# Causal scores of the first 128 queries: high and low key halves as one 256-column product per head, their halves added with the mask on VectorE

## Chip, cores and metric

One core of one Trainium2 chip runs the whole program: two layers of a decoder trunk over 256 tokens. The metric is device time in microseconds (us), the median of several runs of one execution each. The kernel before takes 412.61 us (3 runs, 412.49 to 412.74).

Engines, as the profile names them: PE is TensorE's matmul, PEld its weight load, DVE is VectorE, ACT is ScalarE, POOL is GpSimd, and SP issues most DMAs.

## What is computed

Each layer projects the normalised tokens to seven groups of columns and a gate, runs three branches (block attention, a gated linear recurrence, cross-attention on memory tokens), multiplies by the gate and projects back. The change touches the block attention alone. With 256 tokens and blocks of 256 keys there is one block, so it is causal attention with 8 heads of width 64. Cut to that:

```python
qa = partial_rope(rms_norm(q_a.reshape(B, S, 8, 64), moba_q_norm[l]), positions)
ka = partial_rope(rms_norm(k_a.reshape(B, S, 8, 64), moba_k_norm[l]), positions)
s = jnp.einsum('bhqd,bhld->bhql', qa, ka) * 64 ** -0.5
s = jnp.where(kpos[None, :] <= qpos[:, None], s, -jnp.inf)
o_a = jnp.einsum('bhql,bhld->bhqd', jax.nn.softmax(s, axis=-1), va)
```

## The kernel before

**Precision.** Matmul operands are of type float32r, which keeps fewer bits than float32. So operands are split into a high part (the value cast to float32r) and a low part (the value minus the high part), and a product is the sum of two or three products in PSUM. Every weight chunk (128 x 1024, `wr`) is split so: ACT writes the high part `wh` (line 147), DVE the low part `wl` (line 159). Line 199 is the helper `mm`, through which most products go, so that tiles rather than lines tell them apart.

**Staging.** The main loop walks weight chunks in a fixed order. PE accumulates a projection in `acc` tiles (4 PSUM banks). All else (norms, attention, recurrence) lives in generators, which the main loop advances by a step after each half chunk, and which use `sd` tiles (4 other PSUM banks). A counter `held["sd"]` limits how many `sd` tiles are handed out at a time. The order on each engine is then decided by the framework's scheduler, from the order of the code and its own estimate of durations; at run time each engine works its queue strictly in that order, and an instruction that waits holds up all that is queued behind it.

**The block attention.** `g_qk` makes keys and queries ready: per pair of heads p (4 of them) and parity e (2) the transposed keys, 64 rows per head. For keys (q=1) the high part `kh` and the low part `kl` are written to 64 of 128 partitions and copied by four DMAs on ACT's queue (line 876) to the other 64; for queries the high and low parts lie one above the other in the 128 partitions of `qs`. A product of `qs` (128 rows) with `kh` thus gives (high + low query) times high key, and one with `kl` the same times the low key. `kl` shares its buffers with the output tiles of the memory branch (`yh`, `yl` of branch `M_`), which are written later in a layer.

`g_moba_unit(l, u)` runs once for each parity u, so two units per layer and four in all. It has two steps t, one for each half of the queries:

- t = 0: queries 0 to 127 see keys 0 to 127. For each of 4 heads a 128-column product with `kh` and one with `kl` are summed in PSUM; the 4 heads fill one `sd` tile.
- t = 1: queries 128 to 255 see keys 0 to 255: two 256-column products per head, 4 heads in two `sd` tiles.
- After each step DVE adds the mask `cm` to each head's scores and takes the row maximum in one instruction (line 906; the profile calls it CUSTOM_DVE_ANT_0, and a short READ_ACCUMULATOR follows each). The result goes to `P`.
- Later: the negated scaled maximum `nba` (line 910), the exponentials on ACT (line 919), the reciprocal `ria` of the sums (line 924), the scaling of `P` (line 928), transposes of `P` on PE (line 938), and the product with the values.

Around these steps stand in time the projection of the attention's gate (`acc<-hT,wh` and `acc<-hT,wl`, with `al` copied by ACT at line 282 and `as` added by DVE at line 283), the last levels of the recurrence (`hQ`, `hK`, `hST`, `hX`), and then the projections of the memory gate and of the memory queries.

Of the kernel before, what the change touches and what calls it, by code (L numbers as in the profile page):

```python
# [45 lines left out]
def hymba_kernel(ctx: ExitStack, tc: tile.TileContext, x, mem, mem_t, positions, w_in, w_out, w_mem_kv,  # L46
# [16 lines left out]
    def room(what, n=1):  # L63
        while held[what] + n > room_of[what]:
            yield
# [14 lines left out]
    def rel(what="sd", n=1):  # L80
        held[what] -= n
# [116 lines left out]
    def mm(o, a, b, s, e):  # L198
        nc.tensor.matmul(o, lhsT=a, rhs=b, start=s, stop=e)  # L199
# [482 lines left out]

    def y_tiles(br):
        if f"y{br}" not in T:
            T[f"y{br}"] = [sb.tile([128, 4, 256], F32R, name=f"y{c}{br}", tag=f"y{c}{br}", bufs=1) for c in "hl"]
        return T[f"y{br}"]

    def y_store(l, br, u, po):
# [129 lines left out]
    def g_qk(l, q, acc):  # L818
        ss = small("ssa", 16)
        ms = small("msa", 16)  # L820
        r = small("rka" if q else "rqa", 16)
        kr = sb.tile([128, 2, 512], F32, name="kr", tag="qk", bufs=1)
        for t in range(2):
            t8 = slice(t * 8, t * 8 + 8)
            sumsq(ss[:, t8], acc[t], 8)
            nc.vector.tensor_scalar(ms[:, t8], ss[:, t8], 1.0 / 64, EPS, op0=OP.mult, op1=OP.add)  # L826
            nc.gpsimd.tensor_tensor(r[:, t8], ms[:, t8], pw[:, :8], op=OP.pow)  # L827
            a3 = heads(acc[t], 8)
            k3 = heads(kr[:, t], 8)
            nc.vector.tensor_tensor(k3, a3, rtA[:, l, q, t][:, None, :].to_broadcast([128, 8, 64]), op=OP.mult)  # L830
            tm = sb.tile([128, 8, 16], F32, name="tm", tag="tm", bufs=2)
            nc.vector.tensor_tensor(tm[:, :, 0:8], a3[:, :, 8:16],
                                    rtB[:, l, q, t][:, None, 0:8].to_broadcast([128, 8, 8]), op=OP.mult)
            nc.vector.tensor_tensor(tm[:, :, 8:16], a3[:, :, 0:8],
                                    rtB[:, l, q, t][:, None, 8:16].to_broadcast([128, 8, 8]), op=OP.mult)
            yield
            nc.vector.tensor_tensor(k3[:, :, 0:16], k3[:, :, 0:16], tm, op=OP.add)
            yield
        if q == 0:
            rq = small("rq", 16)  # L840
            nc.gpsimd.tensor_scalar(rq, r, 0.125, None, op0=OP.mult)
            nr = small("nr", 16)
            nc.gpsimd.tensor_scalar(nr, r, -0.125, None, op0=OP.mult)
            T["rq"], T["nr"] = rq, nr
        else:
            yield
            for t in range(2):
                k3 = heads(kr[:, t], 8)
                nc.vector.tensor_tensor(k3, k3, r[:, t * 8:t * 8 + 8][:, :, None].to_broadcast([128, 8, 64]),
                                        op=OP.mult)  # L850
                yield
        yield 2
        halves = (slice(0, 64), slice(64, 128))
        if q:
            hi = [sb.tile([128, 4, 256], F32R, name="kh", tag=f"kh{e}", bufs=1) for e in range(2)]
            lo = [sb.tile([128, 4, 256], F32R, name="kl", tag=f"y{c}{M_}", bufs=1) for c in "hl"]
        else:
            hi = lo = [sb.tile([128, 4, 256], F32R, name="qs", tag=f"y{c}{A_}", bufs=1) for c in "hl"]
        for t in range(2):
            ts = slice(t * 128, (t + 1) * 128)  # L860
            yield from room("sd")
            pt = side_tile()
            for p in range(4):
                nc.tensor.transpose(pt[:, p * 128:(p + 1) * 128], kr[:, t, p * 128:(p + 1) * 128], ident)  # L864
            p3 = heads(pt, 4)
            for e in range(2):
                r = halves[e]
                nc.scalar.copy(hi[e][r, :, ts], p3[r])
                nc.vector.tensor_tensor(lo[e][halves[e if q else 1 - e], :, ts], p3[r], hi[e][r, :, ts].bitcast(F32),
                                        op=OP.subtract)  # L870
            rel()
            yield
        if q:
            for a in (hi, lo):
                for e in range(2):
                    nc.scalar.dma_start(a[e][halves[1 - e]].bitcast(F32), a[e][halves[e]].bitcast(F32))
            T["k2"] = hi, lo
        else:
            T["q2"] = hi
            spawn(g_moba(l))  # L880

    def g_moba_unit(l, u):
        qs, rq, nr = T["q2"][u], T["rq"], T["nr"]
        kh, kl = (a[u] for a in T["k2"])
        yield from room("P")
        held["P"] += 1
        P = sb.tile([128, 4, 384], F32, name="P", tag="P", bufs=2)
        mx = small("mxa%d" % u, 8)
        nb = small("nba%d" % u, 8)
        sm = small("sma%d" % u, 8)  # L890
        ri = small("ria%d" % u, 8)
        kc = (slice(0, 128), slice(128, 384))
        for t in range(2):
            nk = 128 * (t + 1)
            if t:
                yield
            yield from room("sd", t + 1)
            ps = [side_tile() for _ in range(t + 1)]
            ps = [ps[i * nk // 512][:, i * nk % 512:i * nk % 512 + nk] for i in range(4)]
            for i in range(4):  # L900
                for k in (kh, kl):
                    mm(ps[i], qs[:, i, t * 128:(t + 1) * 128], k[:, i, 0:nk], k is kh, k is kl)
            yield
            for i in range(4):
                c = t * 4 + i
                nc.vector.tensor_tensor_reduce(out=P[:, i, kc[t]], in0=ps[i],
                                               in1=cm[:, 256 - nk:], scale=1.0, scalar=-3e38,
                                               op0=OP.add, op1=OP.max, accum_out=mx[:, c:c + 1])
            rel("sd", t + 1)
        nc.vector.tensor_tensor(nb.rearrange("p (t h) -> p t h", t=2), mx.rearrange("p (t h) -> p t h", t=2),  # L910
                                nr.rearrange("p (t h e) -> p t h e", t=2, e=2)[:, :, :, u], op=OP.mult)
        yield
        while u and f"z{M_}{l}" not in done:
            yield
        yield 4
        for t in range(2):
            for i in range(4):
                c, r = t * 4 + i, t * 8 + 2 * i + u
                pin(nc.scalar.activation(P[:, i, kc[t]], P[:, i, kc[t]], AF.Exp, bias=nb[:, c:c + 1],
                                         scale=rq[:, r:r + 1], accum_out=sm[:, c:c + 1]))  # L920
                if i % 2 == 1:
                    yield
        yield
        nc.vector.reciprocal(ri, sm)
        for t in range(2):
            for i in range(4):
                c = t * 4 + i
                nc.vector.tensor_scalar(P[:, i, kc[t]], P[:, i, kc[t]], ri[:, c:c + 1], None, op0=OP.mult)
        yield 2
        tag = ("PTh", "PTl")[u]  # L930
        yield from take(tag)
        PT = sb.tile([128, 4, 384], F32, name="PT", tag=tag, bufs=1)
        for b in range(3):
            bs = slice(b * 128, (b + 1) * 128)
            yield from room("sd")
            pt = side_tile()
            for i in range(4):
                nc.tensor.transpose(pt[:, i * 128:(i + 1) * 128], P[:, i, bs], ident)  # L938
            nc.scalar.copy(PT[:, :, bs], heads(pt, 4))
            rel()  # L940
        rel("P")
        T[f"PT{u}"] = PT
        if u == 0:
            return
        yield 2
        while f"va{l}" not in done or f"z{A_}{l}" not in done:
            yield
        va = T["va"]
        PT = [T.pop(f"PT{e}") for e in range(2)]
        for w in range(2):  # L950
            yield from room("sd")
            po = side_tile()
            for i in range(4):
                p, e = 2 * w + i // 2, i % 2
                h = 2 * p + e
                rows, c = slice(64 * e, 64 * e + 64), (i // 2) * 256
                mm(po[rows, c:c + 256], va[:, 0, h * 64:(h + 1) * 64], PT[e][:, p, 0:256], True, False)
                mm(po[rows, c + 128:c + 256], va[:, 1, h * 64:(h + 1) * 64], PT[e][:, p, 256:384], False, True)
            if w == 0:
                yield  # L960
                y_store(l, A_, w, po)
        rel("PTh")
        rel("PTl")
        yield
        y_store(l, A_, 1, po)
# [234 lines left out]
```

## Time and profile before

| | |
|---|---|
| median of 3 runs | 412.61 us |
| the profiled execution, its own time | 412.44 us |
| its span, first to last instruction | 410.7 us |
| granted TensorE clock, mean | 1.000 |
| products `kh`/`kl` with `qs` of 128 columns | 32 in all, 8 per unit |
| the same of 256 columns | 32 in all, 8 per unit |
| HBM read, written | 66.22 MB, 1.05 MB |

The times of a profiled execution are counted from the start of its span; 1.74 us of its own time lie outside the span. Busy time of PE is no rate: a matmul's row in the trace is longer than the distance to the next matmul's start, since matmuls overlap. What a product costs is therefore read here from starts, or from the chain of waits, which gives back-to-back work as one piece with its whole length. The block attention's scores lie at 113 to 125 us in the first layer and at 313 to 325 us in the second.

### The profile page before, as it was taken

The page shows a single profiled execution, that of the slowest core. Times are in us where ns is not written, and L with a number is a line of the kernel's source. Part 1 is how long each engine was busy: PE and PEld are TensorE (multiplying, and loading weights), DVE is VectorE, ACT ScalarE, POOL GpSimd, SP SyncE. Part 2 cuts the span into 40 slices and gives each one's busy share as a digit, 9 for nine tenths or more (in the row PEclk, how much of TensorE's full clock was granted, in tenths as well). Part 3 has the DMA queues.
Part 4 walks back from the last instruction along what each step waited for, and adds up shares of the span by engine and source line. Part 5 has one row for each costly group of instructions (what it writes and reads, how often), then busy time and mean ns, then how long its engine had stood idle before and what let it go on. Part 6 is the DMA issues. An engine that isn't in the chain of part 4 may idle for free.

```text
span 410.7 us, 7662 instructions
## 1 busy us (share of the span) xinstructions
PE 404.4 (98%) x2940; PEld 338.4 (82%) x2940; DVE 314.6 (77%) x608; ACT 266.6 (65%) x439; POOL 53.1 (13%) x79
## 2 busy tenths in 40 slices
PE   8999999999999999999999999999999999999996
PEld 6788887878899888888878888887888988887885
DVE  4789886788997777876468689659889977678654
ACT  5867864444967999564457666444577599976530
POOL 2005205064001002000000020005400010200000
PEclk9999999999999999999999999999999999999999
DMA  7984666436753444434446555555565434463402
GB/s 253 413 301 134 196 203 194 169 115 213 212 168 119 155 154 155 134 123 153 153 156 204 170 190 166 193 166 174 176 175 188 155 116 143 154 199 107 153 2 102
DMA packets 20261, 69.86 MB, mean 170 GB/s; under 512 B 2560, under 2 KB 2944, under 8 KB 20224
## 3 DMA queue, kind: packets, MB, share of 16 engines
q1 hardware_dynamic: 19296, 67.12, 49.4%
q10 hardware_dynamic: 928, 2.25, 2.2%
q8 instruction: 23, 0.38, 0.4%
q14 instruction: 14, 0.11, 0.1%
HBM read 66.22 MB, written 1.05 MB: 164 GB/s over the span
## 4 chain that ended last, share of the span: by engine, by line
PE 91%; DMA 3%; DVE 3%; ACT 1%; issue 1%; SPq 0%; DVEq 0%
PE acc L199 60%; PE acc L1084 15%; PE sd L199 8%; DMA wr<-in_w_mem_kv_dram 3%; PE sd L203 2%; PE sd L938 1%; PE sd L864 1%; DVE wl L162 1%; PE sd L1047 1%; PE sd L406 1%; ACT wh L150 1%; DVE xs L1118 0%; PE sd L702 0%; PE sd L582 0%; PE sd L993 0%
## 5 line engine op out<-in xcount | busy, mean ns | idle before, releaser
L159 DVE TENSOR_TENSOR wl<-wr,wh 128x1024 fp32r<-128x1024 f32 x104 | 127.1, 1223 | 38.8 <-ACT wh L147 38.3
L147 ACT CAST wh<-wr 128x1024 fp32r<-128x1024 f32 x104 | 109.4, 1052 | 69.7 <-PE acc L199 45.4
L199 PE MATMUL acc<-wh,hT 128*128 128x512 f32 x384 | 122.2, 394 | 0.0
L199 PE MATMUL acc<-hT,wh 128*128 128x512 f32 x256 | 91.5, 398 | 0.3 <-DVE vml L597 0.3
L199 PEld LDWEIGHTS acc<-wh,hT 128*128 128x128 f32 x384 | 71.7, 188 | 14.5
L199 PE MATMUL acc<-wl,hT 128*128 128x512 f32 x192 | 76.2, 397 | 0.0
L199 PE MATMUL acc<-hT,wl 128*128 128x256 f32 x256 | 72.4, 283 | 0.0
L199 PEld LDWEIGHTS acc<-hT,wh 128*128 128x128 f32 x256 | 48.1, 188 | 11.3 <-DVE vml L597 0.7
L199 PEld LDWEIGHTS acc<-hT,wl 128*128 128x128 f32 x256 | 48.4, 189 | 0.2
L199 PEld LDWEIGHTS acc<-wl,hT 128*128 128x128 f32 x192 | 36.1, 188 | 6.9
L1084 PE MATMUL acc<-wl,yh 128*128 128x512 f32 (+1 forms) x96 | 37.3, 394 | 0.0
L1084 PE MATMUL acc<-wh,yl 128*128 128x512 f32 (+1 forms) x96 | 36.9, 393 | 0.0
L1084 PE MATMUL acc<-wh,yh 128*128 128x512 f32 (+1 forms) x96 | 35.2, 397 | 0.0
L162 DVE SCALAR_TENSOR_TENSOR wl<-wr,gT,wh 128x1024 fp32r<-128x1024 f32 (+1 forms) x17 | 20.2, 1220 | 8.7 <-ACT wh L150 8.7
L199 PE MATMUL acc<-wh,mTh 128*128 128x512 f32 x64 | 25.5, 399 | 1.4 <-ACT wh L150 0.9
L150 ACT ACTIVATE wh<-wr,gT 128x1024 fp32r<-128x1024 f32 (+1 forms) x17 | 18.4, 1101 | 12.1 <-PE acc L1084 5.0
L199 PE MATMUL acc<-wh,mTl 128*128 128x512 f32 x64 | 25.0, 390 | 0.0
L827 POOL TENSOR_TENSOR rka<-msa,pw 128x8 f32<-128x8 f32 x4 | 14.2, 3561 | 55.2 <-DVE msa L826 55.2
L1084 PEld LDWEIGHTS acc<-wh,yl 128*128 128x128 f32 x96 | 18.1, 188 | 3.7 <-issue 0.2
L1084 PEld LDWEIGHTS acc<-wl,yh 128*128 128x128 f32 x96 | 18.1, 188 | 3.6 <-issue 0.2
L1084 PEld LDWEIGHTS acc<-wh,yh 128*128 128x128 f32 x96 | 17.9, 188 | 3.8 <-issue 0.3
L199 PE MATMUL acc<-wl,mTh 128*128 128x512 f32 x64 | 20.8, 393 | 0.2 <-DVE wl L162 0.2
(210 smaller groups left out, 615.8 us busy)
## 6 DMA issues: line engine op xcount, KB each, us to landing
wr<-in_w_in_dram SPq DMA_DIRECT2D x80, 512.0 KB, 3.4
wr<-in_w_out_dram SPq DMA_DIRECT2D x24, 512.0 KB, 3.4
wr<-in_w_mem_kv_dram SPq DMA_DIRECT2D x15, 512.0 KB, 3.6
xs<-in_x_dram SPq DMA_DIRECT2D x2, 512.0 KB, 9.2
memr<-in_mem_dram SPq DMA_DIRECT2D x2, 512.0 KB, 6.4
kh<-kh ACTq DMA_DIRECT2D x4, 256.0 KB, 4.5
kl<-kl ACTq DMA_DIRECT2D x4, 256.0 KB, 3.3
out_dram<-xs SPq DMA_DIRECT2D x3, 256.0 KB, 2.0
```

The costliest lines, as they stand in the source:

```text
L147: nc.scalar.copy(whs[i], raws[i])
L150: nc.scalar.activation(whs[i][:, sl], raws[i][:, sl], AF.Copy, scale=gT[:, g:g + 1])
L159: nc.vector.tensor_tensor(wls[i], raws[i], whs[i].bitcast(F32), op=OP.subtract)
L162: nc.vector.scalar_tensor_tensor(wls[i][:, sl], in0=raws[i][:, sl], scalar=gT[:, g:g + 1], in1=whs[i][:, sl].bitcast(F32), op0=OP.mult, op ...
L199: nc.tensor.matmul(o, lhsT=a, rhs=b, start=s, stop=e)
L203: tc.keep_in_program_order(nc.tensor.matmul(o, lhsT=a, rhs=b, start=True, stop=True))
L406: ins = nc.tensor.transpose(pt[:, j * 256 + t * 128:j * 256 + (t + 1) * 128], xn[t][:, k * 128:(k + 1) * 128], ident)
L827: nc.gpsimd.tensor_tensor(r[:, t8], ms[:, t8], pw[:, :8], op=OP.pow)
L864: nc.tensor.transpose(pt[:, p * 128:(p + 1) * 128], kr[:, t, p * 128:(p + 1) * 128], ident)
L938: nc.tensor.transpose(pt[:, i * 128:(i + 1) * 128], P[:, i, bs], ident)
L1047: nc.tensor.transpose(pt[:, i * 256 + t * 128:i * 256 + (t + 1) * 128], P[:, t, i, b * 128:(b + 1) * 128], ident)
L1084: ins = nc.tensor.matmul(a, lhsT=y, rhs=wt[:, cs], start=n == (0 if to is None else nk - 2) and j == 0, stop=n == nk - 1 and j == 2)
```

## The change

The high and low keys of a unit move into one tile `k2` of shape (128, 4 heads, 2 parts, 256 keys): for one head the high part's 256 columns are followed by the low part's 256. At t = 0 one product per head reads columns 0 to 127 of both parts, 256 columns in two runs of 128, and writes (high) and (low) side by side into 256 columns of an `sd` tile. So 4 heads now need two `sd` tiles. For each of them DVE first adds the mask to the low halves of its two heads (a new instruction, 128 partitions x 2 x 128, written to `P`), and the old instruction then adds the high half and `P`, where it added the high half and the mask, and takes the maximum. At t = 1 the same products are computed as before. The DMAs between the halves of the partitions now move 4 runs of 256 floats in each partition where they moved one of 1024. The memory branch's `yh` and `yl` become the halves of one tile `y2` that shares its buffer with the second unit's `k2`.

```diff
     def y_tiles(br):
         if f"y{br}" not in T:
-            T[f"y{br}"] = [sb.tile([128, 4, 256], F32R, name=f"y{c}{br}", tag=f"y{c}{br}", bufs=1) for c in "hl"]
+            if br == M_:
+                y2 = sb.tile([128, 2, 4, 256], F32R, name="y2", tag="y2", bufs=1)
+                T[f"y{br}"] = [y2[:, c] for c in range(2)]
...
         if q:
-            hi = [sb.tile([128, 4, 256], F32R, name="kh", tag=f"kh{e}", bufs=1) for e in range(2)]
-            lo = [sb.tile([128, 4, 256], F32R, name="kl", tag=f"y{c}{M_}", bufs=1) for c in "hl"]
+            k2 = [sb.tile([128, 4, 2, 256], F32R, name="k2", tag=t, bufs=1) for t in ("k2", "y2")]
+            hi, lo = ([a[:, :, c] for a in k2] for c in range(2))
...
-            yield from room("sd", t + 1)
-            ps = [side_tile() for _ in range(t + 1)]
-            ps = [ps[i * nk // 512][:, i * nk % 512:i * nk % 512 + nk] for i in range(4)]
+            yield from room("sd", 2)
+            ps = [side_tile() for _ in range(2)]
             for i in range(4):
-                for k in (kh, kl):
-                    mm(ps[i], qs[:, i, t * 128:(t + 1) * 128], k[:, i, 0:nk], k is kh, k is kl)
+                o, q = ps[i // 2][:, i % 2 * 256:i % 2 * 256 + 256], qs[:, i, t * 128:(t + 1) * 128]
+                if t == 0:
+                    mm(o, q, k2[:, i, :, 0:128], True, True)
+                else:
+                    for c in range(2):
+                        mm(o, q, k2[:, i, c], c == 0, c == 1)
             yield
+            if t == 0:
+                for b in range(2):
+                    nc.vector.tensor_tensor(P[:, 2 * b:2 * b + 2, kc[0]],
+                                            ps[b].rearrange("p (h c s) -> p h c s", h=2, c=2)[:, :, 1],
+                                            cm[:, None, 128:].to_broadcast([128, 2, 128]), op=OP.add)
             for i in range(4):
                 c = t * 4 + i
-                nc.vector.tensor_tensor_reduce(out=P[:, i, kc[t]], in0=ps[i],
-                                               in1=cm[:, 256 - nk:], scale=1.0, scalar=-3e38,
+                o = ps[i // 2][:, i % 2 * 256:i % 2 * 256 + nk]
+                nc.vector.tensor_tensor_reduce(out=P[:, i, kc[t]], in0=o, in1=cm if t else P[:, i, kc[t]],
+                                               scale=1.0, scalar=-3e38,
                                                op0=OP.add, op1=OP.max, accum_out=mx[:, c:c + 1])
-            rel("sd", t + 1)
+            rel("sd", 2)
```

The scheduler orders the engines anew. **PE, first unit of layer 0, before** (out <- operands, the moving tile first; numbers tell tiles of one name apart): the eight 128-column products stand together in tile `sd_1447` within the gate's projection.

```order
L199 MATMUL acc_1481<-hT_159,wh_1324 128x512
L199 MATMUL sd_1447<-kh_1197,qs_1345 128x128
L199 MATMUL sd_1447<-kl_1199,qs_1345 128x128
...
L199 MATMUL acc_1481<-hT_159,wl_1381 128x256
...
L199 MATMUL sd_1490<-kh_1197,qs_1345 128x256
L199 MATMUL sd_1490<-kl_1199,qs_1345 128x256
```

The same place of the changed kernel, down to the first products of the second unit (`k2_1198`):

```order
L199 MATMUL acc_1478<-hT_159,wh_1322 128x512
L199 MATMUL sd_1445<-k2_1197,qs_1343 128x256 x2
L199 MATMUL acc_1478<-hT_159,wl_1379 128x256
...
L199 MATMUL sd_1446<-k2_1197,qs_1343 128x256 x2
L199 MATMUL sd_1487<-k2_1197,qs_1343 128x256 x4
L199 MATMUL sd_1488<-k2_1197,qs_1343 128x256 x4
...
L199 MATMUL sd_1532<-hQ_687,hK_534 128x128 x4
...
L199 MATMUL sd_1544<-k2_1198,qs_1344 128x256 x2
```

Two of the four products of t = 0 (`sd_1445`) stay where the eight were; the other two (`sd_1446`) now stand with those of t = 1. Between the first and the second unit's products 48 `acc` products, 12 `sd` products of 256 columns and the 4 of `hQ`, `hK` are queued. The second unit's `sd_1544` waits for DVE's last reading of `sd_1487`.

**DVE at the same place, before:** after the recurrence's `hK` and a weight split, the four maxima of t = 0 follow one another (a READ_ACCUMULATOR row after each).

```order
L752 TENSOR_TENSOR hK_534<-hK_534,hT32_1385 128x8x64
L159 TENSOR_TENSOR wl_1468<-wr_1322,wh_1416 128x1024
L906 ISA P_1442,mxa0_1443<-sd_1447,cm_162 128x128
...
L283 TENSOR_TENSOR as_1413<-acc_1433,al_1478 128x256
L159 TENSOR_TENSOR wl_1515<-wr_1377,wh_1466 128x1024
L283 TENSOR_TENSOR as_1510<-acc_1481,al_1523 128x256
L906 ISA P_1442,mxa0_1443<-sd_1490,cm_162 128x256
```

**DVE, changed:** the same stretch has the two new additions (line 913), and the maxima of t = 0 (line 919 with `P` as second operand) come in two pairs; the second pair is queued behind t = 1's.

```order
L756 TENSOR_TENSOR hK_534<-hK_534,hT32_1383 128x8x64
L913 TENSOR_TENSOR P_1440<-sd_1445,cm_162 128x2x128
L159 TENSOR_TENSOR wl_1463<-wr_1320,wh_1414 128x1024
L283 TENSOR_TENSOR as_1411<-acc_1431,al_1475 128x256
L919 ISA P_1440,mxa0_1441<-sd_1445,P_1440 128x128
...
L159 TENSOR_TENSOR wl_1512<-wr_1375,wh_1461 128x1024
L283 TENSOR_TENSOR as_1507<-acc_1478,al_1520 128x256
L913 TENSOR_TENSOR P_1440<-sd_1446,cm_162 128x2x128
L919 ISA P_1440,mxa0_1441<-sd_1487,cm_162 128x256
...
L679 TENSOR_TENSOR zT0_169<-as_1411,sg_1497 128x512
L919 ISA P_1440,mxa0_1441<-sd_1446,P_1440 128x128
```

**DVE some 25 us later, changed:** the reciprocal of the first unit's sums, which waits for ACT's exponentials, now stands ahead of the weight split `wl_1770`, and the eight scalings of `P` behind it. Before, that split (`wl_1774`) stood behind the eight scalings.

```order
L159 TENSOR_TENSOR wl_1736<-wr_1612,wh_1697 128x1024
L812 SCALAR_TENSOR_TENSOR zh_168<-sd_1583,hgr_1650,zh_168 128x128 x4
L812 SCALAR_TENSOR_TENSOR zh_168<-sd_1618,hgr_1650,zh_168 128x128 x4
L937 RECIPROCAL ria0_1444<-sma0_1443 128x8
L283 TENSOR_TENSOR as_1694<-acc_1711,al_1747 128x256
L159 TENSOR_TENSOR wl_1770<-wr_1662,wh_1734 128x1024
L941 TENSOR_SCALAR P_1440<-P_1440,ria0_1444 128x128 x4
```

The moves around the reciprocal change the place of DVE's work, not its amount.

More of the change, by code (lines that the diff above doesn't have):

```diff
@@ L684, in y_tiles @@
         if f"y{br}" not in T:
-            T[f"y{br}"] = [sb.tile([128, 4, 256], F32R, name=f"y{c}{br}", tag=f"y{c}{br}", bufs=1) for c in "hl"]
+            if br == M_:
+                y2 = sb.tile([128, 2, 4, 256], F32R, name="y2", tag="y2", bufs=1)
+                T[f"y{br}"] = [y2[:, c] for c in range(2)]
+            else:
+                T[f"y{br}"] = [sb.tile([128, 4, 256], F32R, name=f"y{c}{br}", tag=f"y{c}{br}", bufs=1) for c in "hl"]
         return T[f"y{br}"]
@@ L876, in g_qk @@
                     nc.scalar.dma_start(a[e][halves[1 - e]].bitcast(F32), a[e][halves[e]].bitcast(F32))
-            T["k2"] = hi, lo
+            T["k2"] = k2
         else:
@@ L883, in g_moba_unit @@
         qs, rq, nr = T["q2"][u], T["rq"], T["nr"]
-        kh, kl = (a[u] for a in T["k2"])
+        k2 = T["k2"][u]
         yield from room("P")
@@ L896, in g_moba_unit @@
                 yield
-            yield from room("sd", t + 1)
-            ps = [side_tile() for _ in range(t + 1)]
-            ps = [ps[i * nk // 512][:, i * nk % 512:i * nk % 512 + nk] for i in range(4)]
+            yield from room("sd", 2)
+            ps = [side_tile() for _ in range(2)]
             for i in range(4):
-                for k in (kh, kl):
-                    mm(ps[i], qs[:, i, t * 128:(t + 1) * 128], k[:, i, 0:nk], k is kh, k is kl)
-            yield
+                o, q = ps[i // 2][:, i % 2 * 256:i % 2 * 256 + 256], qs[:, i, t * 128:(t + 1) * 128]
+                if t == 0:
+                    mm(o, q, k2[:, i, :, 0:128], True, True)
+                else:
+                    for c in range(2):
+                        mm(o, q, k2[:, i, c], c == 0, c == 1)
+            yield
+            if t == 0:
[3 more added lines that the diff above has]
+                                            cm[:, None, 128:].to_broadcast([128, 2, 128]), op=OP.add)
             for i in range(4):
                 c = t * 4 + i
-                nc.vector.tensor_tensor_reduce(out=P[:, i, kc[t]], in0=ps[i],
-                                               in1=cm[:, 256 - nk:], scale=1.0, scalar=-3e38,
+                o = ps[i // 2][:, i % 2 * 256:i % 2 * 256 + nk]
+                nc.vector.tensor_tensor_reduce(out=P[:, i, kc[t]], in0=o, in1=cm if t else P[:, i, kc[t]],
+                                               scale=1.0, scalar=-3e38,
                                                op0=OP.add, op1=OP.max, accum_out=mx[:, c:c + 1])
-            rel("sd", t + 1)
+            rel("sd", 2)
         nc.vector.tensor_tensor(nb.rearrange("p (t h) -> p t h", t=2), mx.rearrange("p (t h) -> p t h", t=2),
```

## The prediction

> **What bounds the kernel now.** First the page: busy time, the chain of waits by engine, and the view of who kept PE waiting.
>
> ```profile
> span 410.7 us, 7662 instructions
> PE 404.4 (98%) x2940; PEld 338.4 (82%) x2940; DVE 314.6 (77%) x608; ACT 266.6 (65%) x439; POOL 53.1 (13%) x79
> PEclk9999999999999999999999999999999999999999
> PE 91%; DMA 3%; DVE 3%; ACT 1%; issue 1%; SPq 0%; DVEq 0%
> ...
> PE sd L199 <- DVE dm L325: 1.0, 1, 1.0
> PE acc L199 <- ACT wh L150: 0.9, 2, 0.5
> PE acc L199 <- DVE xs L1118: 0.5, 1, 0.5
> PE acc L199 <- DVE vml L597: 0.3, 1, 0.3
> PE acc L199 <- DVE wl L162: 0.2, 1, 0.2
> ```
>
> PE is busy for 404.4 of 410.7 us, the chain that ended last is PE's own for 91%, and in the whole span PE waited 2.9 us for anybody, none of it for the attention. The granted clock is full in every slice. So what PE no longer executes leaves the end, as long as nobody makes PE wait instead. The busy times by stretch (layer 0; columns PE, PEld, DVE, ACT, POOL, then clock, DMA share, GB/s) show who could:
>
> ```profile
> 108.00:126.00 18.00, 18.00 (x133) 16.18 (x132) 17.78 (x48) 12.55 (x24) 0.00 (x0) 1.00 0.54 167
> 126.00:148.00 22.00, 22.00 (x129) 19.00 (x127) 17.43 (x41) 20.44 (x38) 1.67 (x1) 1.00 0.43 136
> 148.00:160.00 12.00, 12.00 (x58) 9.94 (x57) 6.95 (x10) 11.93 (x25) 2.39 (x2) 1.00 0.48 153
> ```
>
> PE is full in all three. But in the stretch where the change adds work to DVE, DVE is busy for 17.78 of 18.00 us, and ACT is nearly full in the two behind it. These are the places to watch.
>
> **What PE loses.** The chain in order of time (start, length, what) has the eight products of t = 0 of both units, and in between the first unit's eight of t = 1, as pieces of their own:
>
> ```profile
> 113.29 0.84 PE sd L199 x8
> 114.13 3.58 PE acc L199 x20
> 117.71 0.94 PE sd L199 x8
> 118.65 0.46 PE acc L199 x3
> 119.11 0.89 PE sd L199 x8
> 120.00 0.93 PE acc L199 x5
> 120.93 0.84 PE sd L199 x8
> ...
> 312.96 0.84 PE sd L199 x8
> 320.61 0.84 PE sd L199 x8
> ```
>
> Eight products of 128 columns take 0.84 us, 0.105 each; eight of 256 columns take 0.94, 0.117 each. Twice the columns cost a ninth more. The reason stands in the tile's groups: every product has a weight load of its own, of the same 190 ns whatever follows, and these come no closer than about 0.11 us.
>
> ```profile
> L199 PEld LDWEIGHTS sd<-kl,qs x32: 187/189/192, 113.1 to 324.8; 128*128 128x128 f32 x32
> L199 PE MATMUL sd<-kl,qs x32: 272/278/285, 113.2 to 325.0; 128*128 128x128 f32 x16, 128*128 128x256 f32 x16
> ```
>
> Four products of 256 columns take 4 x 0.117 = 0.47 us, so a unit saves 0.84 - 0.47 = 0.37 us, and four units 1.48. From below, the 256 columns now come in two runs of 128, and no row shows a moving operand of that form: if each run cost what a product of its own does, the saving would be 0. From above, a product cannot save more than it costs: 16 x 0.105 = 1.68. I take 1.48, since only 16 of 32 weight loads are left, and the 256-column row is the nearest. Splitting t = 0 into two places costs nothing that the rows show, since `sd` and `acc` products follow each other at every border above without a gap.
>
> Here a rule of the Trainium skill can be held against the rows. Its page "TensorE: Matmul & The Clock Gate", section "Back-to-back issue gap", has an isolated matmul at columns / 2.4 + 2.5 ns: 56 ns for 128 columns and 109 for 256. By it two narrow products cost as much as a wide one but for 2.5 ns, the saving would be 16 x 2.5 ns = 0.04 us (an estimate from that page), and the time would stay. The same page's section "LDWEIGHTS (loading the stationary operand)" has 128 columns / 1.2 = 107 ns for each load, which agrees with the 0.105 of the chain. The rows are on the side of the load.
>
> **What DVE gains.** Four additions per layer of 128 x 256 that read PSUM. The nearest row is line 283, an addition of the same size from PSUM: 418 ns long, 0.34 us from its start to the next.
>
> ```profile
> 117.19 1.22 DVE L159 TENSOR_TENSOR wl<-wr,wh 128x1024 fp32r<-128x1024 f32 x1
> 118.44 0.29 DVE L906 CUSTOM_DVE_ANT_0 P<-sd,cm 128x128 f32<-128x128 f32 x1
> ...
> 118.66 0.28 DVE L906 CUSTOM_DVE_ANT_0 P<-sd,cm 128x128 f32<-128x128 f32 x1
> ...
> 119.29 0.42 DVE L283 TENSOR_TENSOR as<-acc,al 128x256 f32<-128x256 f32 x1
> 119.63 1.22 DVE L159 TENSOR_TENSOR wl<-wr,wh 128x1024 fp32r<-128x1024 f32 x1
> 120.76 0.42 DVE L283 TENSOR_TENSOR as<-acc,al 128x256 f32<-128x256 f32 x1
> 121.10 0.41 DVE L906 CUSTOM_DVE_ANT_0 P<-sd,cm 128x256 f32<-128x256 f32 x1
> ...
> 121.44 0.42 DVE L906 CUSTOM_DVE_ANT_0 P<-sd,cm 128x256 f32<-128x256 f32 x1
> ```
>
> That is 4 x 0.34 = 1.36 us per layer; bounds are 0.21 each (a 128-column maximum, start to start) and 1.13 (a weight split of 1024). I take 0.34. The maxima keep their sizes: only one operand is `P` instead of `cm`. On the path to the end is none of this unless a reader waits.
>
> *The banks.* PE first meets DVE's new order at `sd_1544`, the second unit's first product, which needs the bank that the second maximum of `sd_1487` frees. DVE's queue up to there, from 117.19 and start to start: addition 0.34, split 1.13, `as` 0.34, two maxima 2 x 0.21, split 1.13, `as` 0.34, addition 0.34, two maxima 2 x 0.34: 4.72, so free at 121.9 and some 0.1 for the read-out: 122.0. PE's queue to there, from 113.29: 12 `sd` products x 0.117 = 1.40, the piece of `hQ`, `hK` 0.89, and 48 `acc` products at 3.58 / 20 = 0.18, 8.6: about 124.2, or 124.0 if the chain's pieces lie 0.16 behind the starts. PE comes 2.0 us after DVE is done. Two additions more by 0.79 each (the upper bound) would still fit.
>
> *The weight splits.* After the addition of 1.36 us DVE has idle time to catch up before it is late: rows behind this stretch wait for ACT.
>
> ```profile
> 131.11 0.69 DVE L541 TENSOR_REDUCE ssh<-sq 128x4 f32<-128x512 f32 x1 [1.45 <-ACT sq L540]
> ...
> 142.12 0.20 DVE L924 RECIPROCAL ria<-sma 128x8 f32<-128x8 f32 x1 [1.37 <-ACT P L919]
> ...
> 144.55 1.22 DVE L159 TENSOR_TENSOR wl<-wr,wh 128x1024 fp32r<-128x1024 f32 x1
> ...
> 157.31 1.23 DVE L159 TENSOR_TENSOR wl<-wr,wh 128x1024 fp32r<-128x1024 f32 x1 [1.23 <-ACT wh L147]
> ...
> 159.85 0.39 PE L199 MATMUL acc<-wl,hT 128*128 128x512 f32 x1
> ```
>
> The split at 144.55 is the one that now stands behind the reciprocal; it also passes ahead of eight scalings, which the trace of before has in front of it at 142.72 to 144.55:
>
> ```profile
> 142.72 1.92 DVE L928 TENSOR_SCALAR P<-P,ria 128x128 f32<-128x128 f32 x8
> ```
>
> 1.83 us less and 1.36 more in front of it: it isn't later. The tightest split is the last, at 157.31: it ends at 158.54 and PE takes it up at 159.85, 1.31 us on. It starts when ACT has cast its high part, not when DVE is free, and ACT gets no instruction more. PE comes to it 2 x 0.37 = 0.74 us earlier than before, so 0.57 is left. I cost it at nothing; the cover is thin.
>
> *The key copies.* They now move runs of 1 KB, not 4 KB. The last one that the first unit needs is issued at 104.75, and PE wants it at 113.13: 8.4 us. The slowest of eight took 5.8.
>
> ```profile
> DMA to landing us min/median/max: 3.0/3.5/5.8
> 104.75 0.47 ACTq L876 DMA_DIRECT2D kl<-kl  x1
> 113.13 0.22 PE L199 MATMUL sd<-kh,qs 128*128 128x128 f32 x1
> ```
>
> No row has a copy in 1 KB runs within SBUF; it would have to take 8.4 - 3.5 = 4.9 us more than the median to be seen, so I cost it at nothing. The merged buffers change no order here: `y2` is written long after the second unit's scores, as `yh`, `yl` were.
>
> **The sum**, against the profiled execution: 412.44 - 1.48 + 0 = 410.96 us. That execution lies 0.17 below the median of the runs, so 412.61 - 1.48 = 411.13: I say **411.1**, or 0.36% less. A measurement of this kernel can tell about 0.2%, 0.8 us, from no change.
>
> **Rivals.**
>
> 1. *Late splits.* ACT and DVE lie behind by what DVE gained, and PE waits at the last split of the stretch: 1.36 - 0.57 = 0.8 us per layer, 1.6 in all, which takes the gain back: 412.6 - 1.48 + 1.6 = 412.7. Half of it gives 411.9. With the additions at their upper bound, 4.5 us per layer, DVE would be late by 4.5 - 1.45 - 1.37 - 0.57 = 1.1 per layer, and the time 413.4. For it: DVE full to 99%, ACT to 99%. Against it: DVE's 1.36 falls into a stretch ahead of 1.45 and 1.37 us of idle time.
> 2. *Width is the price.* The two runs cost as two products, or the load hides behind wider columns less well: nothing saved, 412.6. Against it stand 0.84 and 0.94 for eight. The page's rule above would end here too; with eight narrow products at 0.105 instead of 0.056 it has no row on its side.
> 3. *Slower: the banks.* A unit now takes two of four `sd` banks at t = 0 and two at t = 1, and the second unit's matmuls stand in PE's queue ahead of everything. If DVE frees the bank more than 2.0 us later than I add up, PE stands there with all its queue, once per layer. To lose more than 1.48 + 0.8 = 2.3 us it takes 1.15 per layer beyond these 2.0, 3.2 us in all at the second addition. At 3.5 us the time would be 412.6 - 1.48 + 2 x 1.5 = 414.1. For it: strict queues and a full DVE. Against it: no single DVE row of that stretch is longer than 1.23 us.
>
> **Chances.** Forecast, 410.7 to 411.5: 0.68. Late splits, 411.5 to 412.7: 0.14, half of it still below 411.8. Nothing saved: 0.08, of which the page's rule has 0.01. Banks, or another order that makes PE wait by more than the gain: 0.10, nearly all of it slower. The sum could come out lower by the 0.2 that a product can save at most beyond 1.48, and by the run's own spread of 0.1. Faster by over 0.2%: 0.68 + 0.07 = 0.75. Within 0.2%: 0.07 + 0.08 + 0.01 = 0.16. Slower: 0.09. The range of 410.7 to 412.4 holds the forecast and most of the late splits; what it leaves out is about 0.2.
>
> **What the changed kernel's profile would show.** The four pieces of 0.84 gone and 16 products of 256 columns from `k2` at 0.117, PE's busy time less by about 1.5 us: the saving. No wait of PE for `P`, `mxa` or `wl` between 108 and 160 us and between 308 and 360: the cover. DVE more by 2.7 us of spacing, eight additions of about 0.42 us in their rows. The four key copies landing within 8 us. Wrong would be: PE's starts 0.2 us apart at `k2`, which is rival 2; PE waiting for `wl` near 158 or 357, rival 1; for a maximum near 124 or 323, rival 3. If PE's busy time falls by 1.5 us and the span doesn't, the loss lies elsewhere than I looked.

## The result, and the profile after

| | before | after |
|---|---|---|
| median of 4 runs each | 412.68 us (412.49 to 412.84) | 410.00 us (409.76 to 410.21) |
| the profiled execution, its own time | 412.44 us | 410.15 us |

The ratio is 0.9935, with a 95% interval of 0.9918 to 0.9952: 2.7 us less by the medians, 2.29 by the profiled executions. The forecast was 411.1, the sum for the profiled execution 410.96. The profiled execution lies 0.81 us below that sum, and the median of 410.00 below the low end of the range, 410.7.

The page of the changed kernel (span; engines; the chain of waits by engine), and who kept PE waiting:

```profile
span 408.4 us, 7640 instructions
PE 402.2 (98%) x2924; PEld 336.7 (82%) x2924; DVE 316.3 (77%) x616; ACT 266.6 (65%) x439; POOL 54.3 (13%) x79
PE 91%; DMA 3%; DVE 3%; ACT 1%; issue 1%; SPq 0%; DVEq 0%; ACTq 0%
...
PE sd L199 <- DVE dm L325: 1.0, 1, 1.0
PE acc L199 <- ACT wh L150: 0.8, 2, 0.4
PE acc L199 <- DVE xs L1131: 0.5, 1, 0.5
PE acc L199 <- DVE vml L597: 0.4, 1, 0.4
PE acc L199 <- DVE wl L162: 0.2, 1, 0.2
```

The five waits of PE are those of before, 2.9 us in all as then. So no wait came, and none went. DVE is busy for 1.7 us more (314.6 before). But PE's busy time fell by 404.4 - 402.2 = 2.2 us, where 1.5 was forecast. PE lost more work time than the edited products have to give, or did other work faster.

Where? Both kernels execute the same wide products (into `acc`) in nearly the same sequence, so the start of the product at the same place of that sequence can be read in both timelines. Four such starts serve as landmarks. PE, layer 0, before (start, length, engine, line, operation, tiles, count):

```profile
110.67 0.40 PE L199 MATMUL acc<-hT,wh 128*128 128x512 f32 x1
...
169.91 0.40 PE L1084 MATMUL acc<-wl,yh 128*128 128x512 f32 x1
...
177.61 0.39 PE L1084 MATMUL acc<-wl,yh 128*128 128x512 f32 x1
...
184.66 0.84 PE L1084 MATMUL acc<-wh,yh 128*128 128x512 f32 x3
```

The same four products in the changed kernel:

```profile
110.73 0.40 PE L199 MATMUL acc<-hT,wh 128*128 128x512 f32 x1
...
169.18 0.40 PE L1097 MATMUL acc<-wl,yh 128*128 128x512 f32 x1
...
176.37 0.39 PE L1097 MATMUL acc<-wl,yh 128*128 128x512 f32 x1
...
183.49 0.85 PE L1097 MATMUL acc<-wh,yh 128*128 128x512 f32 x3
```

From the first to the second lie the scores: 59.24 us before, 58.45 after, 0.79 less. From the second to the third lies the product of the probabilities with the values, PT·va, which the change doesn't edit: 7.70 before, 7.19 after, 0.51 less. Behind it 0.07 is lost again (7.05 and 7.12). In layer 1 the four starts lie as far apart, to 0.01 us. So the edited products gave about what was forecast, and a second gain of about 0.5 us per layer stands 50 us later, with another product.

The scores first. The chain in order of time, changed kernel:

```profile
113.35 0.23 PE sd L199 x2
...
117.59 1.18 PE sd L199 x10
...
124.13 0.24 PE sd L199 x2
```

Ten products of 256 columns, two of them merged ones, take 1.18 us, 0.118 each; the merged ones that stand alone in pairs take the same, 0.23 for two. Now PT·va. PE's timeline before, and the ACT copy that feeds it the last piece of `PT`:

```profile
172.11 0.86 PE L199 MATMUL sd<-PT,va 128*64 128x256 f32 x6
172.91 0.50 PE L1084 MATMUL acc<-wl,yh 128*128 128x512 f32 x1
173.24 0.39 PE L1084 MATMUL acc<-wh,yl 128*128 128x512 f32 x1
...
174.26 2.38 PE L199 MATMUL sd<-PT,va 128*64 128x128 f32 x26
176.58 0.50 PE L1084 MATMUL acc<-wh,yh 128*128 128x512 f32 x1
...
170.60 0.60 ACT L939 COPY PT<-sd 128x512 f32<-128x512 f32 x1
```

The changed kernel:

```profile
172.92 0.39 PE L1097 MATMUL acc<-wh,yl 128*128 128x512 f32 x1
173.23 2.87 PE L199 MATMUL sd<-PT,va 128*64 128x256 f32 x32
176.04 0.50 PE L1097 MATMUL acc<-wh,yh 128*128 128x512 f32 x1
```

Each of the 16 products of a layer leaves two records here, so "x6" and "x26" are 3 and 13 products. Before, the scheduler cut PT·va behind the third product and put five products of the output projection (`w_out` in the expectations below) in between. After, all 16 stand in one piece. The queue shows where the cut comes from (rows of PE before, with numbers and waits):

```
837 L199 MATMUL sd_2112<-PT_1785,va_2049 64x256 [waits DVE_49,Activation_49]
838 L199 MATMUL sd_2112<-PT_1785,va_2049 64x128
839 L199 MATMUL sd_2112<-PT_1986,va_2049 64x256
840 L1084 MATMUL acc_2052<-wl_2030,yh1_1781 128x512
...
844 L1084 MATMUL acc_2053<-wh_1982,yl1_1782 128x512
845 L199 MATMUL sd_2112<-PT_1986,va_2049 64x128 [waits Activation_49]
```

The fourth product is the one that waits for ACT's last copy of `PT`. Presumably the scheduler, by its own estimate of durations, filled that wait; the estimate itself is in no trace. On the chip there was none: the copy ended at 171.20, 1.7 us before the cut. In the changed kernel's order the cut is gone.

What the cut costs can be added up from starts. Before: 172.91 - 172.11 = 0.80 for the first piece, 176.58 - 174.26 = 2.32 for the second, 3.12 in all; the five products between take 174.26 - 172.91 = 1.35 where five at 0.23 take 1.15. After: 176.04 - 173.23 = 2.81 for the whole. So the cut costs 0.31 in PT·va and 0.20 in the wide products between, 0.10 at either end of them (172.91 to 173.24, and 0.32 from the start of the last one to 174.26): 0.51 us per layer, as between the two landmarks.

### The profile page after: what moved, and what is told of

It reads as the page before. It is cut to its first block, busy times and chain, and to the rows that moved or that the text cites. A ratio compares the mean times of both kernels' runs of the same rounds, so it can differ in the third digit from the quotient of the medians.

```text
span 408.4 us, 7640 instructions
## 1 busy us (share of the span) xinstructions
PE 402.2 (98%) x2924; PEld 336.7 (82%) x2924; DVE 316.3 (77%) x616; ACT 266.6 (65%) x439; POOL 54.3 (13%) x79
## 4 chain that ended last, share of the span: by engine, by line
PE 91%; DMA 3%; DVE 3%; ACT 1%; issue 1%; SPq 0%; DVEq 0%; ACTq 0%
PE acc L199 61%; PE acc L1097 15%; PE sd L199 7%; DMA wr<-in_w_mem_kv_dram 3%; PE sd L203 2%; PE sd L951 1%; PE sd L868 1%; DVE wl L162 1%; PE sd L1060 1%; PE sd L406 1%; ACT wh L150 1%; DVE xs L1131 0%; PE sd L706 0%; PE sd L582 0%; PE sd L1006 0%
## 5 line engine op out<-in xcount | busy, mean ns | idle before, releaser
L1097 PE MATMUL acc<-wl,yh 128*128 128x512 f32 x64 | 25.7, 402 | 0.0
L1097 PE MATMUL acc<-wh,yl 128*128 128x512 f32 x64 | 25.1, 392 | 0.0
L1097 PE MATMUL acc<-wh,yh 128*128 128x512 f32 x64 | 23.6, 404 | 0.0
L1097 PE MATMUL acc<-wh,y 128*128 128x512 f32 (+1 forms) x64 | 20.2, 388 | 0.0
L932 ACT ACTIVATE P<-P,nba,rq 128x128 f32<-128x128 f32 (+1 forms) x32 | 17.3, 545 | 0.1
L199 PEld LDWEIGHTS acc<-wh,mTh 128*128 128x128 f32 x64 | 12.1, 189 | 5.0 <-ACT wh L150 1.7
```

The lines of the kernel that those rows point to most:

```text
L1097: ins = nc.tensor.matmul(a, lhsT=y, rhs=wt[:, cs], start=n == (0 if to is None else nk - 2) and j == 0, stop=n == nk - 1 and j == 2)
```

## The experiments

Three theories. **A, the cut:** the merged products give 1.50 us in both layers, and the vanished cut of PT·va 0.98 (the landmarks have 1.58 and 1.02). **B, the products:** all of it comes from the merged products, their banks or their layout. **C, knock-on:** PT·va got shorter because it starts earlier, whatever its order. Theory A was read off the two traces; the runs below undo either term by itself.

One measure serves all of them: the stretch on PE in layer 0 from the first to the last of the four landmarks above (73.99 us before, 72.76 after). In every kernel it holds the same products but for the scores that the change edits. Its reading in layer 1 agrees within 0.01 us for every kernel, while whole times move by some tenths with the start of the program (the first landmark alone lies between 110.38 and 111.43 us in these runs). Each ratio is to runs of before in the same round: the first to fourth kernels ran beside 18 with a median of 412.50 us, the fifth to seventh on another chip beside 17 with 413.27, so that medians are not to be set against those of another round. Each stretch is read from one profiled execution.

| kernel | t = 0 products | PT·va in pieces of | stretch, us | median, us | ratio to before, 95% |
|---|---|---|---|---|---|
| before | 128 columns | 3, 13 | 73.99 | 412.68 | 1 |
| after | 256 | 16 | 72.76 | 410.00 | 0.9935 (0.9918 to 0.9952) |
| first: before, one piece | 128 | 16 | 73.41 | 411.24 | 0.9964 (0.9951 to 0.9978) |
| second: after, cut | 256 | 3, 13 | 73.20 | 411.09 | 0.9968 (0.9956 to 0.9981) |
| third: after, narrow | 128 | 3, 13 | 74.10 | 412.69 | 1.0007 (0.9998 to 1.0016) |
| fourth: after, narrow, one piece | 128 | 16 | 73.45 | 411.42 | 0.9974 (0.9964 to 0.9985) |
| fifth: after, two cuts | 256 | 3, 5, 8 | 73.63 | 411.94 | 0.9977 (0.9968 to 0.9986) |
| sixth: after, late cut | 256 | 12, 4 | 73.12 | 411.00 | 0.9950 (0.9938 to 0.9962) |
| seventh: after, other order | 256 | 16 | 72.38 | 410.21 | 0.9926 (0.9914 to 0.9939) |

**First: the kernel before with PT·va in one piece.**

```diff
-        for b in range(3):
+        for b in (2, 0, 1):
             bs = slice(b * 128, (b + 1) * 128)
...
-            for i in range(4):
+            for i in (1, 0, 3, 2):
                 p, e = 2 * w + i // 2, i % 2
```

> The kernel before, with its old scores. Only the order of the PT copies (third key block first) and of the two heads of a pair in PT·va is turned round, so that all sixteen PT·va products of a layer come ready together and stand in one piece on PE, where the kernel before has 3, then five w_out products, then 13. Theory A (the cut): the traces of before and after differ by 0.75 us a layer in the scores and by 0.49 us a layer in the stretch with PT·va, and the second is the price of the cut; so this kernel saves 2 x 0.49 = 0.98 us without the change: about 411.5 in a profiled run where before shows 412.4. Theory B (all of the gain comes from the merged products, their banks or their layout): no change, 412.4. Theory C (PT·va got shorter because the scores end earlier, whatever the order): no change, 412.4.

Measured 411.24, in a ratio of 0.9964 where A's 0.98 us is 0.9976. The chain has the whole of PT·va as one piece, as long as in the changed kernel, though it holds the old scores:

```profile
176.31 2.80 PE sd L199 x32
```

The stretch is 0.58 us shorter than before's. B and C fall: nearly half of the gain of 1.23 per layer is to be had without touching a score, and with PT·va later than before, not earlier. But the 0.58 isn't the cut alone: the turned order moves other small pieces too, and in the seventh experiment, where there is no cut to remove, it shortens the stretch by 0.22 to 0.38.

**Second: the changed kernel with PT·va cut again.** A pause in the code before the fourth product and an order edge bring other work in between. The second product of each head now has a line of its own, 973, but is the same product.

```diff
                 mm(po[rows, c:c + 256], va[:, 0, h * 64:(h + 1) * 64], PT[e][:, p, 0:256], True, False)
-                mm(po[rows, c + 128:c + 256], va[:, 1, h * 64:(h + 1) * 64], PT[e][:, p, 256:384], False, True)
+                if w == 0 and i == 1:
+                    yield 5
+                ins = nc.tensor.matmul(po[rows, c + 128:c + 256], lhsT=va[:, 1, h * 64:(h + 1) * 64],
+                                       rhs=PT[e][:, p, 256:384], start=False, stop=True)
+                if w == 0 and i == 1:
+                    pin(ins)
```

> The kernel after, with the merged products, but PT·va cut again after its third product (pieces of 3 and 13, other work between). Theory A: the 0.98 us come back, about 411.1 where after shows 410.15; the score stretch stays as short as in after. Theories B and C: no change, 410.15.

Measured 411.09, as A said, in a ratio of 0.9968; its interval lies above that of the changed kernel in the table and overlaps that of the changed kernel's second round, 0.9934 to 0.9962. The chain shows the first three products as 0.59 + 0.20 = 0.79 us again, and other work behind:

```profile
173.43 0.59 PE sd L199 x4
174.01 0.20 PE sd L973 x2
174.22 3.67 PE acc L1102 x15
```

The stretch from the first landmark to the second is 58.45 as in after; all the loss lies behind it, 0.44 us net.

**Third: two products of 128 columns again, all else as changed** (layout, copies, banks, additions).

```diff
-                    mm(o, q, k2[:, i, :, 0:128], True, True)
+                    for c in range(2):
+                        mm(o[:, c * 128:c * 128 + 128], q, k2[:, i, c, 0:128], True, True)
```

> The kernel after, but each merged product of the first 128 queries is two products of 128 columns into the same places of the same banks; VectorE's work is as in after. The scheduler cuts PT·va into 3 and 13 here, as in before. Theory A: both terms come back, 1.50 for the width and 0.98 for the cut, 410.15 + 2.48 = 412.6. Theory B with the price in the products: also about 412.4 (2.29 back), but with the time in the score rows: each unit would cost 0.57 more there, not 0.37. Theory C: 412.4. Told apart by the score stretch (0.75 a layer by A and C) and by the next kernel.

Measured 412.69, the time of before: both terms are gone, and nothing else of the change has a price that shows in the time (its stretch is 0.11 longer than before's). From the first landmark to the second it takes 59.34, 0.89 more than the changed kernel, where A said 0.75 and B 1.14; this reading alone would not part the two. In its chain the first unit's four narrow products stand as 0.40 us (two merged ones: 0.23), and PT·va is in two pieces:

```profile
113.00 0.40 PE sd L199 x4
...
172.46 0.80 PE sd L199 x6
173.26 1.13 PE acc L1098 x4
174.38 2.31 PE sd L199 x20
```

That also shows what removes the cut: between this kernel and the changed one only the width of these products differs in the code, and the scheduler cuts PT·va in the one and not in the other.

**Fourth: narrow products, PT·va in one piece** (the edits of the third and of the first together).

> As the kernel with two narrow products, with the PT·va order of the first experiment, which puts its sixteen products in one piece. Theory A: only the width is lost, 410.15 + 1.50 = 411.65. Theories B and C: as without that order, about 412.4.

Measured 411.42. Piece and stretch agree with the first experiment, which has the old layout and banks:

```profile
176.33 2.80 PE sd L199 x32
```

The changed kernel and the second, third and fourth have both widths, cut and whole, and make a square. By stretches the width is worth 74.10 - 73.20 = 0.90 us per layer with the cut and 73.45 - 72.76 = 0.69 without it; the cut is worth 74.10 - 73.45 = 0.65 with narrow products and 73.20 - 72.76 = 0.44 with wide ones. The two readings of each term differ by 0.2. The square isn't clean: the fourth kernel has the turned order of the first experiment and the changed kernel has not, and the order of other small pieces moves each time too (among them the transposes of `P`). Against the seventh kernel, which has the fourth's order with the merged products, the width is worth 0.92 to 1.07. Single terms are no better known from whole stretches than that.

**Fifth: two cuts.** As the second, with `yield 3` for `yield 5`.

> The kernel after with PT·va in three pieces a layer (3, 5 and 8 products) and w_out products between them. If the price is one of each cut: two cuts in each of two layers, 4 x 0.49 = 1.96 us, 410.15 + 1.96 = 412.1. If only the first interruption costs (a state that is lost once), about 411.1, as with one cut. If the cut isn't the cause, 410.15.

Measured 411.94; the stretch grew by 0.87 per layer, twice the second experiment's 0.44. By its ratio the time doesn't decide: 0.9977 lies between 0.9992 (412.1 / 412.44, two cuts) and 0.9968 (411.1 / 412.44, one). But it is 0.94 longer than the sixth kernel, which has one cut and ran in the same round; by the stretches the second cut asks 2 x 0.51 = 1.02. So the price is one of each cut, not of the first alone.

**Sixth: a cut between pairs.** A pause behind the first two pairs of each tile, of which the scheduler made one cut, behind the twelfth product.

```diff
                 mm(po[rows, c + 128:c + 256], va[:, 1, h * 64:(h + 1) * 64], PT[e][:, p, 256:384], False, True)
+                if i == 1:
+                    yield
```

> The kernel after with PT·va cut once a layer, but between two pairs (12 products, three w_out products, 4 products) instead of inside a pair as in the kernel before. If the price is one of leaving and coming back at any place: two cuts at 0.49, about 411.1. If it is the broken pair (the second product of a head standing alone at the front of the next piece): about 410.15, or some tenths above.

Measured 411.00. Its ratio of 0.9950 can't be told from the changed kernel's; its stretch is longer by 0.36. From the chain:

```profile
173.44 2.15 PE sd L199 x24
175.60 0.90 PE acc L1099 x3
176.49 0.81 PE sd L199 x8
```

The pieces sum to 2.96 against 2.80 whole, 0.16 more; the three wide products take 0.90 against 0.69, 0.21 more. So by the rows 0.36 of the price is for leaving and coming back between pairs; the other 0.15 of the cut in before, which costs PT·va 0.31 and not 0.16, is what a break inside a pair adds.

**Seventh: the order of the first experiment in the changed kernel.**

> The kernel after with the order of the first experiment (third key block first, heads of a pair turned round). PT·va is in one piece already, so by the cut alone nothing changes: 410.15. The new order also puts the transposes of P into fewer pieces (37 pieces of transposes that end in front of wider work in the whole program, 43 in after). A piece of transposes in after's trace costs the wide product behind it 0.08 us, so six fewer would save 0.5: about 409.6. If pieces of transposes cost nothing on balance: 410.15.

Measured 410.21, and its profiled run 409.63. PT·va is as long as in after, and the stretch 0.38 us shorter. By the ratio it can't be told from the changed kernel, so it was run again beside that.

> The kernel after, unchanged, on the chip of the next run, to compare the two: about 2.3 us less than before there (0.9945 of it), by the two terms of 1.50 and 0.98.

> The seventh kernel once more. Between the same wide products of the two traces a layer took 0.33 us less than in after, outside the start of the program, so 0.66 us in both layers; if that holds in the times, 0.6 us less than after on the same chip (0.9985 of it). If the start of the program decides, no difference that can be told.

The changed kernel: 410.15 (409.87 to 410.19), ratio 0.9948 (0.9934 to 0.9962). The other order: 409.58 (409.41 to 410.17), ratio 0.9937 (0.9923 to 0.9951); its stretch was 72.53 this time (0.15 longer than in its first execution), that of after 72.75. It is the lowest median of all, but the intervals overlap: that it beats the changed kernel isn't settled, nor which of the moved pieces would do it.

## Why the prediction was wrong

**What bounds the kernel: right.** PE still sets the end, and its waits in all are the same 2.9 us.

**The width: right.** A merged product takes 0.118 us, forecast 0.117. Eight per layer take 0.94 where sixteen narrow ones took 1.68: 0.74 per layer, 1.48 in both, the forecast to the digit; between the landmarks, with what else moved there, it is 0.79. The two runs of columns cost nothing extra. The formula of the page "TensorE: Matmul & The Clock Gate", section "Back-to-back issue gap" of the Trainium skill, by which two narrow products cost no more than a wide one but for 2.5 ns, doesn't hold for these products: width alone is worth 0.69 to 1.07 us per layer by the stretches above. The page gives it for an isolated matmul and says itself that at few columns it counts too little, because it leaves out the weight load; so the prediction had set up a rival that the page doesn't support. That two places for t = 0 cost nothing is right too: the pair at 113.35 takes 0.23 between wide products.

**DVE, the banks and the splits: right.** The additions are as long as forecast, the bank that the second unit needs is read by 122.15 (forecast 122.0), and PE comes at 124.13 (124.0 to 124.2).

```profile
L913 DVE TENSOR_TENSOR P<-sd,cm x8: 412/418/425, 117.4 to 325.3; 128x256 f32<-128x256 f32 x8
...
121.73 0.42 DVE L919 CUSTOM_DVE_ANT_0 P<-sd,cm 128x256 f32<-128x256 f32 x1
...
157.08 1.23 DVE L159 TENSOR_TENSOR wl<-wr,wh 128x1024 fp32r<-128x1024 f32 x1 [0.19 <-ACT wh L147]
...
159.10 0.39 PE L199 MATMUL acc<-wl,hT 128*128 128x512 f32 x1
```

The tightest split ends at 158.31 and is taken up at 159.10: 0.79 us of slack, forecast 0.57. DVE's busy time rose by 1.7 us where 2.7 of spacing was forecast; no new wait for DVE came.

**The key copies: right.** In runs of 1 KB they land after 3.9 us in the median and 6.2 at most, within the 8.4 that were there:

```profile
DMA to landing us min/median/max: 3.0/3.9/6.2
```

**The sum: wrong, and here is the step.** "412.44 - 1.48 + 0" had a term for each edited instruction and a 0 for everything else. The prediction looked at where the new order could make PE wait, and nowhere, beyond the places of t = 0, at whether the same PE work costs the same in another order: that was put at 0 without a reason. It doesn't cost the same: PT·va, 50 us behind the edit, went from two pieces to one, 0.51 us per layer. The two layers' stretches between the landmarks give 412.44 - 2 x 1.23 = 409.98 (0.79 + 0.51 - 0.07 per layer); the 0.17 up to 410.15 lies outside them, at the start and between the layers.

**The range: wrong for the same reason.** Its low end let the sum fall by the 0.2 that the products could give at most beyond 1.48, and held no term for reordered work, though the order of both kernels could have shown the cut. The signal that the forecast named for itself did its work: PE's busy time fell by 2.2 instead of 1.5, with no wait changed, which points to other PE work that became cheaper.

None of the three rivals came: no late split, no price for the width, no wait for a bank.

## What to carry to other kernels

Where a scheduler orders the queues, an edit's cost is not the edited instructions alone: compare the two orders on the engine that sets the end over the whole program, and price each place where a run of small products is cut or joined. Where one engine is full, measure between the starts of the same two instructions in both traces; these stretches agree to 0.01 us between the layers of an execution, and did so between two executions of the changed kernel, where whole times move by tenths. Two executions of the seventh kernel differed by 0.15, so one reading is no proof of a tenth. A cut that the scheduler made for a wait which the trace doesn't show can be taken out by hand: here that, with the other pieces that the turned order moved, gave the kernel before 0.58 us per layer.

## What had not been expected of the hardware

Leaving a piece of PT·va for wide products and coming back costs PE 0.36 us, and 0.51 where the cut falls inside a pair. It shows in the first wide product behind a piece (row of 0.50 us, next start 0.33 later, not 0.23), in the last one ahead of it (0.32), and in the pieces themselves. The products of the memory branch, with all 128 columns of weights and the split operands, pay nothing for a cut. Chain of before, then of after:

```profile
170.53 0.71 PE sd L199 x6
171.25 0.23 PE acc L1084
```

```profile
170.50 1.42 PE sd L199 x12
```

Before, six of these take 0.71, one wide product 0.23, and six more follow; after, the twelve take 1.42, twice 0.71. PT·va differs from them in two ways, 64 columns of weights where they have 128, and float32 operands with two records per product, where they are float32r. No run varied one of the two alone, but other pieces in the same traces have one without the other. The transposes of `P` are float32 with 128 columns of weights; before, the first wide product behind them starts at 169.59 and the next at 169.91, 0.32 later, while the wide product ahead of them takes 0.23 (169.01 to 169.24):

```profile
169.01 0.39 PE L1084 MATMUL acc<-wh,yl 128*128 128x512 f32 x1
169.24 0.60 PE L938 MATMUL sd<-ident,P 128*128 128x128 f32 x4
169.59 0.48 PE L1084 MATMUL acc<-wh,yh 128*128 128x512 f32 x1
```

The recurrence's products have fewer than 128 columns of weights in their early levels, and there the wide product ahead takes 0.32 to 0.33, as ahead of PT·va; ahead of its float32 products with 128 columns (`hST`) it takes 0.23 to 0.24. One of each, from before and from the changed kernel:

```profile
111.73 0.40 PE L199 MATMUL acc<-hT,wh 128*128 128x512 f32 x1
112.06 0.69 PE L203 MATMUL sd<-hQ,hK 128*64 128x64 f32 x16
```

```profile
131.33 0.40 PE L199 MATMUL acc<-hT,wh 128*128 128x512 f32 x1
131.56 0.38 PE L199 MATMUL sd<-ih,hST 128*128 128x128 f32 x2
```

So in these traces the price behind a piece goes with float32, and the price ahead of it with fewer than 128 columns.

The break inside a pair has a cause of its own that the trace of the second experiment shows. The two heads of a pair write different halves of the 128 output partitions, and their products run side by side. The second piece there begins with the left-over product (line 973) and the next pair's first (line 199) at the same time:

```profile
177.82 0.32 PE L973 MATMUL sd<-PT,va 128*64 128x128 f32 x1
177.82 0.43 PE L199 MATMUL sd<-PT,va 128*64 128x256 f32 x1
```

The products of the memory branch start 0.12 apart instead. A pair of four products takes 0.70 in one piece (2.80 / 4); the first three alone take 0.79, since one head's second product then runs with nothing beside it.
